# Three of four groups of a feed-forward projection computed as seven products of halves

## The chip, the core and the metric

The kernel runs on one core of one Trainium2 chip. The metric is the device time of one execution in microseconds (us): the median of several runs, lower is better. The engines are TensorE (PE; its weight loads are shown as PEld), VectorE (DVE), ScalarE (ACT), GpSimd (POOL) and SyncE (SP), whose queue here issues all DMA transfers. Each engine works through its own list of instructions in order; semaphores tie the lists together.

## The reference, cut to what matters

The model has two layers of width 1024 on 512 tokens, all in float32. Each layer mixes three branches (sparse attention, retention, a convolution) and ends with a feed-forward part, the only one that the change touches:

```python
for l in range(2):
    ...                                   # mixer: x = x + merged @ w_out[l]
    h2 = _rmsnorm(x, norm_mlp[l])         # (512, 1024)
    x = x + jnp.square(jax.nn.relu(h2 @ w_ff1[l])) @ w_ff2[l]   # 1024 -> 4096 -> 1024
return _rmsnorm(x, norm_final)
```

## The kernel before, in words

Activations lie transposed: a tile is 128 channels by 512 tokens, and `xT` is a list of eight of them. For float32 accuracy each operand of a product is split in a high part and the rest (`split`, lines 111 to 113: ScalarE rounds a copy `hi`, VectorE subtracts it from the source to give `lo`), and each product is three matmuls: high by high, high by low, low by high. A block of a projection (`proj`, lines 158 to 165) is one output tile of 128 channels: it goes over eight pieces k of 128 input channels, 24 matmuls of 512 columns into one PSUM tile `mm` (three buffers). Its weights come as one load of 512 KB into a tile `wr` (three buffers), are copied to `wh` by ScalarE (L145) and subtracted to `wl` by VectorE (L150 in this stage; elsewhere by GpSimd, L148).

The feed-forward stage (lines 795 to 819) has its operand `X` from `norm_split`: eight high/low pairs of `xT` times the gain of the norm; the row factor `rs` follows later and is multiplied in when a block is drained. The 4096 hidden channels are worked in four groups `q` of eight blocks. For each group the first projection makes eight blocks from `X` and `w_1`, each drained by VectorE (L806: relu, times `rs`), squared by ScalarE (L807) and split into a pair of hidden tiles; these lie in tiles `fa` of the stage's own pool in groups 0 and 2, and in tiles `bo` and `kv` of the mixer's pool in groups 1 and 3. Then the second projection makes eight blocks from `w_2` and the eight hidden pairs, and VectorE adds each to `xT[m]` (L817).

A scheduler of the framework puts each engine's instructions in an order of its own, from its own estimate of when each can start; tiles of one tag share a fixed number of buffers, and an instruction that takes a buffer again waits for its last reader.

Of the kernel before, what the change touches and what calls it, by code (L numbers as in the profile page):

```python
# [66 lines left out]
def block_kernel(ctx: ExitStack, tc: tile.TileContext, a, out):  # L67
    nc = tc.nc
    consts = ctx.enter_context(tc.tile_pool(name="consts", bufs=1))
    base = ctx.enter_context(tc.tile_pool(name="base", bufs=1))  # L70
# [12 lines left out]
    def tl(pool, tag, bufs, shape=(P, T), dtype=F):  # L83
        count[0] += 1
        return pool.tile(list(shape), dtype, name=f"{tag}_{count[0]}", tag=tag, bufs=bufs)

    def new_pool(name, side="left"):
        return tc.tile_pool(name=name, bufs=1, side=side, reuse_waits="tile")

    def tmp(shape=(P, T), dtype=F):  # L90
        return tl(base, "t", 3, shape, dtype)

    def small(shape, dtype=F):
        if math.prod(shape[1:]) <= 8:
            return tl(base, "n", 40, shape, dtype)
        return tl(base, "m", 7, shape, dtype)
# [11 lines left out]
    def mm(o, l, r, start, stop):  # L108
        return nc.tensor.matmul(o, l, r, start=start, stop=stop)  # L109

    def split(hi, lo, src, eng=None):
        nc.scalar.activation(hi, src, AF.Copy)
        return (eng or nc.vector).tensor_sub(lo, src, f(hi))
# [22 lines left out]
    def raw(srcs, nk, n):  # L136
        t = tl(base, "wr", 3, (P, nk, n))
        for dst, src in srcs(t):
            dma(dst, src)
        return t  # L140

    def wsplit(t, nk, n):
        h = tl(base, "wh", 3, (P, nk, n), FR)
        l = tl(base, "wl", 3, (P, nk, n), FR)
        nc.scalar.activation(h, t, AF.Copy)  # L145
        if lo_engine[0] is nc.gpsimd:
            for k in (slice(0, nk // 2), slice(nk // 2, nk)):
                nc.gpsimd.tensor_sub(l[:, k], t[:, k], f(h[:, k]))  # L148
        else:
            nc.vector.tensor_sub(l, t, f(h))  # L150
        return h, l

    def wblock(src, nk=KC, n=P):

        return wsplit(raw(lambda t: [(t, src)], nk, n), nk, n)

    def proj(o, w, x, nk=KC):

        h, l = w
        for k in range(nk):  # L160
            xh, xl = x[k]
            mm(o, h[:, k, :], xh, k == 0, False)
            mm(o, h[:, k, :], xl, False, False)
            last = mm(o, l[:, k, :], xh, False, k == nk - 1)
        return last
# [70 lines left out]
    first = start.enter_context(new_pool("first"))  # L236
    xT = [tl(first, "x0", 8) for _ in range(KC)]
    w_first = tl(base, "wr", 3, (P, KC, P))
    dma(pcol, a["cols"][:, 0:P])
    for c in range(KC):  # L240
        if c < 2:
            k = slice(4 * c, 4 * c + 4)
# [22 lines left out]
        for h in range(HEADS):  # L265
            dma(fd[h], f1[h:h + 1, :].to_broadcast([P, FLEN]))

    NR = 64
    open_pools = start
    for l in range(DEPTH):  # L270
        b = l * NR
        par = lambda at, n=1: pcol[:, b + at:b + at + n]
        w_f, w_t = a["w_f"][l], a["w_t"][l]

        if l == 0:
            h, lo = tl(base, "wh", 3, (P, KC, P), FR), tl(base, "wl", 3, (P, KC, P), FR)
# [3 lines left out]
        X, rs4, rs = norm_split(xT, par(0, 8), l == 0)  # L280
# [13 lines left out]
        def bo():  # L294
            return tl(mix_pool, "bo", 8, dtype=FR)

        def kv(shape=(P, T)):
            return tl(mix_pool, "kv", 12, shape, FR)
# [21 lines left out]
        def conv_taps_behind(ins, n):  # L320
            with tc.issue_after(ins.ins):
                conv_taps(n)
# [28 lines left out]
        for which, c0 in (("q", 0), ("k", 2)):  # L351
# [3 lines left out]
            for i in range(NB):  # L355
                z = pz[i].rearrange("p (h s d) -> p h s d", s=2, d=32)
                cosb = cs[:, i, None, None, 0:32].to_broadcast([P, 4, 2, 32])
                sinb = cs[:, i, None, 32:64].to_broadcast([P, 4, 32])
                A = tl(rp, "rr", 8, (P, 4, 2, 32))
                B = tmp((P, 4, 2, 32))  # L360
                nc.vector.tensor_mul(A, z, cosb)
                nc.vector.tensor_mul(B[:, :, 0, :], z[:, :, 1, :], sinb)
                nc.vector.tensor_mul(B[:, :, 1, :], z[:, :, 0, :], sinb)
                nc.vector.tensor_sub(A[:, :, 0, :], A[:, :, 0, :], B[:, :, 0, :])  # L364
                rotated = nc.vector.tensor_add(A[:, :, 1, :], A[:, :, 1, :], B[:, :, 1, :])
                rr.append(A)
                conv_taps_behind(rotated, T_ROT)
            for c in range(2):
# [4 lines left out]
                for s in range(2):  # L373
                    h = 2 * c + s
# [13 lines left out]
        for h in range(4):  # L388
            if h % 2 == 0:
# [16 lines left out]
            t = tmp()  # L406
# [7 lines left out]
            at = [slice(c, c + T - j * P) for j, c in enumerate((0, 512, 896, 1152))]  # L414
            for j in range(NB):
                n = T - j * P
                s = ps("sc")
                mm(s[:, :n], KSr[h][:, j * P:(j + 1) * P], QHr[h][:, j * P:], True, False)
                mm(s[:, :n], KSr[h][:, j * P:(j + 1) * P], QLr[h][:, j * P:], False, True)
                t = tl(rp, "rt", 2)  # L420
                nc.vector.tensor_mul(t[:, :n], s[:, :n], dec[:, :n])
                conv_taps_behind(split(ph[:, at[j]], pl[:, at[j]], t[:, :n]), T_SCORE)
            o = ps("av")
# [128 lines left out]
        for br, fb in ((0, FB_KS), (1, FB_KW)):  # L552
            pz = ps("mm")
            proj(pz, wblock(w_f[fb]), X)
            t = tmp()
# [13 lines left out]
        for i in range(NB):  # L569
# [4 lines left out]
                                                 op1=OP.subtract)  # L574
# [5 lines left out]
        def ut(dtype=F):  # L580
            return tl(cp, "u", 4, (P, T + CW - 1), dtype)[:, :T]
# [184 lines left out]
        for j in range(HPG):  # L766
            h, lo = tl(pp, "os", 8, dtype=FR), tl(pp, "os", 8, dtype=FR)
# [13 lines left out]
        for m in range(KC):  # L781
            h, lo = (bo(), bo()) if m < 4 else (kv(), kv())
            split(h, lo, merged[m])
            MG.append((h, lo))
        xT = []
        for m in range(KC):
            po = ps("mm")
            proj(po, wblock(a["w_o"][l, m]), MG)
            t = tl(a2, "on", 4) if m < 4 else tl(cp, "yc", 4)
# [7 lines left out]
        fp = phase.enter_context(new_pool(f"ff{l}"))  # L797
        X, rs4, rs = norm_split(xT, par(8, 8))
        lo_engine[0] = nc.vector
        for q in range(4):  # L800
            A = []
            for m in range(KC):
                pf = ps("mm")
                proj(pf, wblock(a["w_1"][l, q * KC + m]), X)
                t = tmp()
                nc.vector.scalar_tensor_tensor(t, pf, 0.0, rs, op0=OP.max, op1=OP.mult)  # L806
                nc.scalar.activation(t, t, AF.Square)  # L807
                if q % 2 == 0:
                    h, lo = tl(fp, "fa", 16, dtype=FR), tl(fp, "fa", 16, dtype=FR)
                else:  # L810
                    h, lo = (bo(), bo()) if m < 4 else (kv(), kv())
                split(h, lo, t)
                A.append((h, lo))
            for m in range(KC):
                pf = ps("mm")
                proj(pf, wblock(a["w_2"][l, q, m]), A)
                nc.vector.tensor_add(xT[m], xT[m], pf)  # L817
        phase.close()
        lo_engine[0] = nc.gpsimd

# [2 lines left out]
    for c in range(KC - 1):  # L823
        s = tmp()
# [4 lines left out]
    s = tmp()  # L829
# [59 lines left out]
```

## Time and profile before

| | |
|---|---|
| median of 3 runs | 1791.85 us (1791.27 to 1793.62) |
| profiled execution | 1793.25 us, span of its instructions 1791.5 us |
| TensorE busy | 1750.2 us, 98% of the span, granted clock 0.989 |
| VectorE, ScalarE, GpSimd busy | 1101.9, 775.0 and 504.8 us |
| feed-forward stages in the chain | 343.64 us from 564.49 us (layer 0), 343.97 us from 1437.13 us (layer 1) |

The span runs from the first to the last instruction; the execution's own time is 1.75 us longer. A matmul's own duration in the profile overlaps its neighbours', so the pace of TensorE is read from the starts of matmuls, not from their lengths. The same holds for VectorE and ScalarE where instructions stand queued.

### The profile page before, as it was taken

The page shows a single profiled execution, that of the slowest core. Times are in us where ns is not written, and L with a number is a line of the kernel's source. Part 1 is how long each engine was busy: PE and PEld are TensorE (multiplying, and loading weights), DVE is VectorE, ACT ScalarE, POOL GpSimd, SP SyncE. Part 2 cuts the span into 40 slices and gives each one's busy share as a digit, 9 for nine tenths or more (in the row PEclk, how much of TensorE's full clock was granted, in tenths as well). Part 3 has the DMA queues.
Part 4 walks back from the last instruction along what each step waited for, and adds up shares of the span by engine and source line. Part 5 has one row for each costly group of instructions (what it writes and reads, how often), then busy time and mean ns, then how long its engine had stood idle before and what let it go on. Part 6 is the DMA issues. An engine that isn't in the chain of part 4 may idle for free.

```text
span 1791.5 us, 23230 instructions
## 1 busy us (share of the span) xinstructions
PE 1750.2 (98%) x8592; PEld 1469.7 (82%) x8592; DVE 1101.9 (62%) x1979; ACT 775.0 (43%) x1421; POOL 504.8 (28%) x420
## 2 busy tenths in 40 slices
PE   8899899999999999999999999999999999999997
PEld 7788788887888888888898888888778888888886
DVE  6976978776764344434459768878768443434344
ACT  4433466675443232323434344667644442323241
POOL 4454444322581000000255544343327500000000
PEclk9999999999999999999999999999999999999999
DMA  4222623321553232333322232232236332332321
GB/s 166 89 86 64 198 95 107 112 95 65 205 184 105 94 94 94 96 95 101 133 101 89 89 119 92 95 126 98 83 122 227 122 94 95 94 96 93 106 85 69
DMA packets 70801, 195.82 MB, mean 109 GB/s; under 512 B 8944, under 2 KB 9328, under 8 KB 70688
## 3 DMA queue, kind: packets, MB, share of 16 engines
q1 hardware_dynamic: 70688, 194.34, 33.5%
q8 instruction: 68, 1.11, 0.3%
q14 instruction: 45, 0.37, 0.1%
HBM read 177.51 MB, written 19.42 MB: 110 GB/s over the span
## 4 chain that ended last, share of the span: by engine, by line
PE 68%; issue 20%; DVE 10%; ACT 1%; DMA 1%; SPq 0%; POOL 0%; POOLq 0%; DVEq 0%; ACTq 0%
PE mm L109 59%; PE sc L109 3%; PE av L109 3%; DVE yc L338 3%; PE tp L722 2%; PE tp L109 1%; DVE qk L386 1%; DVE XP L500 0%; DVE pc L684 0%; DVE rr L364 0%; DVE QS L657 0%; DVE s L712 0%; DVE pt L728 0%; DVE g L448 0%; DVE kv L563 0%
## 5 line engine op out<-in xcount | busy, mean ns | idle before, releaser
L109 PE MATMUL mm<-X,wh 128*128 128x512 f32 x2432 | 779.5, 396 | 12.5 <-ACT X L214 6.0
L148 POOL TENSOR_TENSOR wl<-wr,wh 128x512 fp32r<-128x512 f32 (+2 forms) x344 | 440.1, 1302 | 542.8 <-ACT wh L145 526.8
L145 ACT ACTIVATE wh<-wr 128x1024 fp32r<-128x1024 f32 (+2 forms) x301 | 296.0, 986 | 650.9 <-PE mm L109 522.1
L109 PEld LDWEIGHTS mm<-X,wh 128*128 128x128 f32 x2432 | 456.0, 190 | 102.2 <-ACT X L214 6.0
L109 PE MATMUL mm<-X,wl 128*128 128x512 f32 x1216 | 480.7, 395 | 0.0
L109 PEld LDWEIGHTS mm<-X,wl 128*128 128x128 f32 x1216 | 230.5, 190 | 45.3
L338 DVE SCALAR_TENSOR_TENSOR yc<-u,ccol,yc 128x512 f32<-128x512 f32 x240 | 213.0, 889 | 1.5
L150 DVE TENSOR_TENSOR wl<-wr,wh 128x1024 fp32r<-128x1024 f32 x129 | 158.1, 1226 | 38.2 <-ACT wh L145 38.2
L109 PE MATMUL mm<-bo,wh 128*128 128x512 f32 x512 | 160.6, 392 | 0.0
L109 PE MATMUL mm<-fa,wh 128*128 128x512 f32 x512 | 160.2, 395 | 0.0
L806 DVE SCALAR_TENSOR_TENSOR t<-mm,rs 128x512 f32<-128x512 f32 x64 | 43.9, 691 | 161.6 <-PE mm L109 156.1
L206 POOL TENSOR_TENSOR n<-n,mhalf 128x4 f32<-128x4 f32 x15 | 17.4, 1159 | 371.9 <-DVE n L204 371.9
L227 POOL TENSOR_TENSOR t<-t,t 128x512 f32<-128x512 f32 x18 | 27.4, 1523 | 333.7 <-DVE wl L150 314.4
L109 PE MATMUL mm<-kv,wh 128*128 128x512 f32 x384 | 119.7, 390 | 0.0
L109 PEld LDWEIGHTS mm<-fa,wh 128*128 128x128 f32 x512 | 96.1, 188 | 23.2
L109 PEld LDWEIGHTS mm<-bo,wh 128*128 128x128 f32 x512 | 96.1, 188 | 19.5
L728 DVE TENSOR_TENSOR pt<-tp,pt 128x256 fp32r<-128x256 f32 (+1 forms) x192 | 71.2, 375 | 65.0 <-ACT pt L727 64.3
L109 PE MATMUL mm<-fa,wl 128*128 128x512 f32 x256 | 100.6, 395 | 0.0
L109 PE MATMUL mm<-bo,wl 128*128 128x512 f32 x256 | 100.0, 391 | 0.0
L714 ACT ACTIVATE s<-s,n 128x128 f32<-128x128 f32 (+3 forms) x128 | 71.3, 558 | 43.9 <-DVE n L712 43.4
L109 PE MATMUL mm<-wh,X 128*128 128x256 f32 (+1 forms) x480 | 90.2, 287 | 0.0
L727 ACT ACTIVATE pt<-tp 128x256 fp32r<-128x256 f32 (+1 forms) x192 | 63.7, 340 | 58.6 <-PE tp L722 42.6
(219 smaller groups left out, 2417.9 us busy)
## 6 DMA issues: line engine op xcount, KB each, us to landing
wr<-in_w_dram SPq DMA_DIRECT2D x128, 512.0 KB, 3.6
wr<-in_w_f_dram SPq DMA_DIRECT2D x87, 512.0 KB, 3.3
wr<-in_w_b_dram SPq DMA_DIRECT2D x48, 256.0 KB, 2.7
wr<-in_w_t_dram SPq DMA_DIRECT2D x16, 512.0 KB, 3.4
gd<-g SPq DMA_DIRECT2D x32, 256.0 KB, 2.0
g<-gd SPq DMA_DIRECT2D x32, 256.0 KB, 4.1
wr<-in_w_o_dram SPq DMA_DIRECT2D x16, 512.0 KB, 3.6
md<-g SPq DMA_DIRECT2D x16, 256.0 KB, 2.9
```

What stands on the lines that cost most here:

```text
L109: return nc.tensor.matmul(o, l, r, start=start, stop=stop)
L145: nc.scalar.activation(h, t, AF.Copy)
L148: nc.gpsimd.tensor_sub(l[:, k], t[:, k], f(h[:, k]))
L150: nc.vector.tensor_sub(l, t, f(h))
L227: (nc.vector if c == KC - 1 or first_time else nc.gpsimd).tensor_add(s, s, acc)
L338: nc.vector.scalar_tensor_tensor(yc[c], x, w, yc[c], op0=OP.mult, op1=OP.add)
L386: nc.vector.tensor_sub(QLr[h][half], pt[nat], f(QHr[h][nat]))
L714: nc.scalar.activation(s, s, AF.Exp, scale=-1.0, bias=mx[:, i:i + 1], accum_out=den[:, i:i + 1])
L722: nc.tensor.transpose(pt[:, k * P:(k + 1) * P], cols[i][:, k * P:(k + 1) * P], ident)
L727: nc.scalar.activation(vh, src, AF.Copy)
L728: low = nc.vector.tensor_sub(vl, src, f(vh))
L806: nc.vector.scalar_tensor_tensor(t, pf, 0.0, rs, op0=OP.max, op1=OP.mult)
```

## The change

Group 0 of the first projection stays as it was. Groups 1, 2 and 3 are computed with a scheme of seven products of halves in place of eight (Strassen's in Winograd's form). The operand of a pair of blocks is cut in two: the input channels (`X[0:4]` and `X[4:8]`; of a weight block `lower` and `upper`) and the tokens (`left` and `right`, 256 each); the two output blocks of the pair are the two halves of the output channels. Each product has four pieces k, 12 matmuls of 256 columns, and goes into a PSUM tile of the tags `sc` and `tp` (two buffers each), which are free in this stage.

- `input_sums` makes, once per layer and beside group 0, the sums of the quarters of the operand, split into tiles `T`; the fourth sum overwrites the right halves of `X[0:4]` after group 0 has read them (`late`).
- `seven(q, p)` is a pair of blocks. It loads both raw weight blocks r1 and r2 into `wr`; r1 is split as before into `wh` and `wl` (A11 and A12 are its halves); VectorE makes four sums of weights in tiles `u` (128x512 each), and S1 to S4 and A22 (the upper half of r2) are split into pieces, 11 tiles of tags `kv` and `W` in rotation. Of the seven products ScalarE copies the first out of PSUM (`g`), and VectorE adds up the others into two output tiles (`t`), seven additions of 128x256. `done` then drains each as before.
- It is a generator: a pair's first four products stand ahead of the second projection's block m of the group before, two more behind that block, and the last behind block m + 1. So the first projection of group q + 1 is dealt out among the blocks of the second projection of group q.
- The hidden pairs lie in a ring of 30 tiles (14 `fa`, 8 `bo`, 8 `kv`).

```diff
+        spare = [kv() for _ in range(4)] + [tl(fp, "W", 7, dtype=FR) for _ in range(7)]
...
+        ring = [tl(fp, "fa", 14, dtype=FR) for _ in range(14)] + [bo() for _ in range(8)] + [kv() for _ in range(8)]
...
+        TS, late, kept = [], [], [ut(), ut()]
+
+        def input_sums(c):
+            b1, b2, s1, s2 = tl(base, "g", 3), tl(base, "g", 3), tmp(), tmp()[:, left]
+            nc.scalar.activation(b1, xT[c], AF.Copy, scale=par(8 + c))
+            nc.scalar.activation(b2, xT[c + 4], AF.Copy, scale=par(12 + c))
+            nc.vector.tensor_sub(s1[:, left], b1[:, right], b1[:, left])
+            nc.vector.tensor_sub(s1[:, right], b2[:, right], s1[:, left])
+            nc.vector.tensor_sub(s2, b2[:, right], b1[:, right])
+            h, lo = (tl(fp, "T", 8, (P, 3, HALF), FR) for _ in range(2))
+            last = kept[c // 2][:, (left, right)[c % 2]]
+            nc.vector.tensor_sub(last, b2[:, left], s1[:, right])
+            split(h[:, 0:2], lo[:, 0:2], s1)
+            split(h[:, 2], lo[:, 2], s2)
...
+            late.append((TS[-1][3], last))
+
+        def seven(q, p):
...
+            r1, r2 = (raw(lambda t: [(t, a["w_1"][l, q * KC + 2 * p + d])], KC, P) for d in range(2))
+            h1, l1 = wsplit(r1, KC, P)
+            s1, s2, s3, s4 = (ut().rearrange("p (k n) -> p k n", n=P) for _ in range(4))
...
+            def both(name, src):
+                W[name] = piece(), piece()
+                split(*W[name], src)
+
+            nc.vector.tensor_add(s1, r2[:, lower], r2[:, upper])
+            both("S1", s1)
+            nc.vector.tensor_sub(s2, s1, r1[:, lower])
+            both("S2", s2)
+            nc.vector.tensor_sub(s3, r1[:, lower], r2[:, lower])
+            nc.vector.tensor_sub(s4, r1[:, upper], s2)
+            both("S3", s3)
+            both("S4", s4)
+            both("A22", r2[:, upper])
...
+            def product(tag, w, B):
+                o = ps(tag)[:, :HALF]
+                h, lo = W[w]
+                for k, (bh, bl) in enumerate(B):
+                    mm(o, h[:, k], bh, k == 0, False)
+                    mm(o, h[:, k], bl, False, False)
+                    mm(o, lo[:, k], bh, False, k == 3)
+                return o
+
+            def done(y):
+                nc.vector.scalar_tensor_tensor(y, y, 0.0, rs, op0=OP.max, op1=OP.mult)
+                nc.scalar.activation(y, y, AF.Square)
+                h, lo = hidden_pair()
+                split(h, lo, y)
+                return h, lo
...
+            nc.scalar.activation(p1, product("sc", "A11", plain(0, left)), AF.Copy)
+            p5 = product("tp", "S1", turned(0))
+            add(y1[:, left], p1, product("sc", "A12", plain(4, left)))
+            add(u2, p1, product("tp", "S2", turned(1)))
+            add(u4, u2, p5)
+            yield
+            p7 = product("sc", "S3", turned(2))
+            add(u3, u2, p7)
+            add(y2[:, right], u4, p7)
+            add(y1[:, right], u4, product("tp", "S4", plain(4, right)))
+            out = [done(y1)]
+            yield
+            add(y2[:, left], u3, product("sc", "A22", turned(3)))
+            yield out + [done(y2)]
+
+        A = []
+        for m in range(KC):
+            A.append(first(0, m))
+            if m % 2:
+                input_sums(m // 2)
+        for (h, lo), t in late:
+            split(h, lo, t)
         for q in range(4):
-            A = []
-            for m in range(KC):
...
+            after = []
+            for m in range(0, KC, 2):
+                part = seven(q + 1, m // 2) if q < 3 else iter([None, None, []])
+                next(part)
+                second(q, m, A)
+                next(part)
+                second(q, m + 1, A)
+                after += next(part)
+            A = after
```

The changed lines move instructions on all engines, as the built programs show. Before, VectorE's list in this stage was, for a block of the second projection, the addition to `xT` (`on` or `yc`) and the `wl` of a later block, and nothing else:

```order
L817 TENSOR_TENSOR on_5162<-on_5162,mm_5789 128x512
L150 TENSOR_TENSOR wl_5889<-wr_5886,wh_5888 128x1024
L817 TENSOR_TENSOR on_5197<-on_5197,mm_5821 128x512
L150 TENSOR_TENSOR wl_5921<-wr_5918,wh_5920 128x1024
L817 TENSOR_TENSOR on_5232<-on_5232,mm_5853 128x512
```

Now 25 instructions stand there for two blocks. The rows below are the turn from one pair to the next in the middle of group 1 of layer 0 (L829 and L150: addition to `xT` and a `wl`; `kv_5488<-wr_7096`: the low half of A22 of the next pair; L911 and L890: the last addition and the drain of the pair at hand; L867 to L871: the weight sums S1 to S3 of the pair after next; L902 and L903: additions of products, `g` being half tiles of sums).

```order
L829 TENSOR_TENSOR on_5267<-on_5267,mm_7044 128x512
L150 TENSOR_TENSOR wl_7249<-wr_7246,wh_7248 128x1024
L113 TENSOR_TENSOR kv_5488<-wr_7096,kv_5487 128x512
L911 TENSOR_TENSOR t_6922<-g_6920,sc_7076 128x256
L890 SCALAR_TENSOR_TENSOR t_6922<-t_6922,rs_5478 128x512
L867 TENSOR_TENSOR u_7303<-wr_7297 128x512
L902 TENSOR_TENSOR g_7120<-g_7120,tp_7165 128x256
L113 TENSOR_TENSOR fa_5505<-t_6922,fa_5504 128x512
L869 TENSOR_TENSOR u_7304<-u_7303,wr_7295 128x512
L871 TENSOR_TENSOR u_7305<-wr_7295,wr_7297 128x512
L903 TENSOR_TENSOR g_7121<-g_7120,tp_7138 128x256
L113 TENSOR_TENSOR W_5490<-u_7303,W_5489 128x512
```

The sums of weights, which read raw tiles `wr`, now stand between additions that drain PSUM tiles. On the SP queue the loads follow each other as r1, r2 of a pair and the two blocks of the second projection beside it.

The second place is VectorE at the end of group 0 of layer 0, where the first pair of group 1 begins (`u_5899`: the fourth weight sum of the first pair, which reads its r1, `wr_5888`; L820: the drain of group 0's last block; L839 to L844: input sums of the last `c`; `wl_6043`: weights of the second projection's block 1; `W_5494<-wr_5890`: the low half of A22, from r2; `wl_6094`: the r1 of the second pair, `wr_6089`).

```order
L872 TENSOR_TENSOR u_5899<-wr_5888,u_5897 128x512
L820 SCALAR_TENSOR_TENSOR t_5859<-mm_5828,rs_5478 128x512
L839 TENSOR_TENSOR t_5866<-g_5864 128x256
L841 TENSOR_TENSOR t_5867<-g_5865,g_5864 128x256
L150 TENSOR_TENSOR wl_6043<-wr_6040,wh_6042 128x1024
L113 TENSOR_TENSOR W_5492<-u_5899,W_5491 128x512
...
L113 TENSOR_TENSOR W_5494<-wr_5890,W_5493 128x512
L113 TENSOR_TENSOR bo_5511<-t_5859,bo_5510 128x512
...
L113 TENSOR_TENSOR T_5874<-t_5867,T_5873 128x256
L150 TENSOR_TENSOR wl_6094<-wr_6089,wh_6093 128x1024
L113 TENSOR_TENSOR T_5874<-t_5866,T_5873 128x512
```

Before, two blocks' drains and splits and the first `wl` of the second projection stood there. The third place is TensorE a little later, within the first pair. Before, a second-projection block's 24 matmuls stood together; now the fourth k of the products S1 (`tp_5932`) and S2 (`tp_5959`), which reads the last `T` (`T_5873`), stands behind most of block 0 (`mm_5974`) and five matmuls of S3 (`sc_6006`).

```order
L109 MATMUL mm_5974<-bo_5510,wh_5977 128x512
L109 MATMUL sc_6006<-T_5609,W_5489 128x256
L109 MATMUL sc_6006<-T_5610,W_5489 128x256
L109 MATMUL sc_6006<-T_5609,W_5490 128x256
L109 MATMUL sc_6006<-T_5697,W_5489 128x256
L109 MATMUL sc_6006<-T_5698,W_5489 128x256
L109 MATMUL tp_5932<-T_5873,kv_5485 128x256
L109 MATMUL tp_5959<-T_5873,kv_5487 128x256
L109 MATMUL mm_5974<-bo_5511,wh_5977 128x512
```

Outside the two feed-forward stages TensorE's list is unchanged.

## Rows read from the trace of the kernel before

**Rows 1.** Page, head: busy us (share of the span) xinstructions of each engine.
```profile
PE 1750.2 (98%) x8592; PEld 1469.7 (82%) x8592; DVE 1101.9 (62%) x1979; ACT 775.0 (43%) x1421; POOL 504.8 (28%) x420
```

**Rows 2.** Chain that ended last, feed-forward of both layers: start us, us, engine, line.
```profile
564.49 343.64 PE mm L109 x1504
...
1437.13 343.97 issue
```

**Rows 3.** Stretches of layer 1's feed-forward: a first-projection group, a second-projection group.
```profile
core 0: us, PE busy (x) PEld busy (x) DVE busy (x) ACT busy (x) POOL busy (x), PEclk, DMA share, GB/s
...
1527.00:1569.00 42.00, 42.00 (x187) 34.81 (x186) 19.25 (x23) 16.24 (x22) 0.00 (x0) 1.00 0.28 88
1570.00:1612.00 42.00, 42.00 (x187) 34.81 (x186) 15.97 (x17) 9.67 (x10) 0.00 (x0) 1.00 0.33 101
```

**Rows 4.** Waits, layer 1's feed-forward: who for whom, us in total, times, longest.
```profile
DVE t L806 <- PE mm L109: 78.1, 29, 3.4
DVE yc L817 <- PE mm L109: 53.6, 16, 3.5
```

**Rows 5.** Timeline of TensorE, 512 and 256 columns: start us, us, instructions merged.
```profile
1454.67 0.62 PE L109 MATMUL mm<-X,wh 128*128 128x512 f32 x2
...
1455.35 0.62 PE L109 MATMUL mm<-X,wh 128*128 128x512 f32 x2
...
918.50 0.40 PE L109 MATMUL sc<-wh,X 128*128 128x256 f32 x2
...
918.86 0.40 PE L109 MATMUL sc<-wh,X 128*128 128x256 f32 x2
```

**Rows 6.** Timeline of VectorE, layer 1's feed-forward: drains and splits.
```profile
1442.87 1.89 DVE L806 SCALAR_TENSOR_TENSOR t<-mm,rs 128x512 f32<-128x512 f32 x3 [2.78 <-ACT rs L231]
...
1446.80 1.90 DVE L113 TENSOR_TENSOR fa<-t,fa 128x512 fp32r<-128x512 f32 x3 [0.85 <-ACT fa L112]
...
1465.75 0.69 DVE L806 SCALAR_TENSOR_TENSOR t<-mm,rs 128x512 f32<-128x512 f32 x1 [2.69 <-PE mm L109]
...
1487.98 0.69 DVE L817 TENSOR_TENSOR on<-on,mm 128x512 f32<-128x512 f32 x1 [3.51 <-PE mm L109]
...
1493.58 0.69 DVE L817 TENSOR_TENSOR on<-on,mm 128x512 f32<-128x512 f32 x1 [3.51 <-PE mm L109]
...
1586.71 0.69 DVE L817 TENSOR_TENSOR yc<-yc,mm 128x512 f32<-128x512 f32 x1 [3.35 <-PE mm L109]
...
1592.15 0.69 DVE L817 TENSOR_TENSOR yc<-yc,mm 128x512 f32<-128x512 f32 x1 [3.35 <-PE mm L109]
```

**Rows 7.** Groups by shape, VectorE in layer 1's feed-forward: busy us, mean ns.
```profile
L150 DVE TENSOR_TENSOR wl<-wr,wh 128x1024 fp32r<-128x1024 f32 x60 | 73.5, 1226 | 13.1 <-ACT wh L145 13.1
...
L113 DVE TENSOR_TENSOR fa<-t,fa 128x512 fp32r<-128x512 f32 x16 | 10.9, 691 | 0.9 <-ACT fa L112 0.9
```

**Rows 8.** Groups by shape, VectorE in the whole run, one of 256 elements.
```profile
L728 DVE TENSOR_TENSOR pt<-tp,pt 128x256 fp32r<-128x256 f32 x128 | 53.7, 419 | 46.8 <-ACT pt L727 46.2
```

**Rows 9.** Groups by shape, ScalarE in layer 1's feed-forward.
```profile
L145 ACT ACTIVATE wh<-wr 128x1024 fp32r<-128x1024 f32 x60 | 63.7, 1062 | 220.8 <-PE mm L109 220.8
L807 ACT ACTIVATE t<-t 128x512 f32<-128x512 f32 x32 | 19.6, 618 | 0.0
L112 ACT ACTIVATE fa<-t 128x512 fp32r<-128x512 f32 x16 | 9.9, 630 | 0.4
```

**Rows 10.** DMA issues in layer 1's feed-forward: KB each, median us to landing.
```profile
wr<-in_w_dram SPq DMA_DIRECT2D x57, 512.0 KB, 3.5
```

**Rows 11.** Page, DMA queues: packets, MB, share of 16 engines' span.
```profile
q1 hardware_dynamic: 70688, 194.34, 33.5%
```

**Rows 12.** DMA issues from 181 to 184 us, loads issued back to back.
```profile
w<-in_cmp_w_k_dram SPq DMA_DIRECT2D x2, 512.0 KB, 6.0
```

**Rows 13.** Timeline of TensorE, end of its longest idle stretch.
```profile
206.32 1.13 PE L109 MATMUL mm<-X,wh 128*128 128x512 f32 x2 [4.69 <-ACT G L575]
```

**Rows 14.** Stretches with a lower granted clock (columns as in rows 3).
```profile
206.50:209.80 3.30, 3.30 (x8) 2.55 (x9) 3.30 (x7) 1.67 (x5) 2.51 (x2) 0.50 1.02 328
...
1083.70:1090.50 6.80, 6.80 (x31) 6.70 (x31) 6.61 (x11) 1.62 (x5) 2.07 (x3) 0.50 0.57 186
```

More of the change, by code (lines that the diff above doesn't have):

```diff
@@ L266, in late_setup @@
             dma(fd[h], f1[h:h + 1, :].to_broadcast([P, FLEN]))
-    NR = 64
+    NR, HALF = 64, T // 2
     open_pools = start
@@ L799, in block_kernel @@
         lo_engine[0] = nc.vector
-        for q in range(4):
-            A = []
-            for m in range(KC):
[L803 to L817, printed above, removed]
+        left, right, lower, upper = slice(0, HALF), slice(HALF, T), slice(0, 4), slice(4, 8)
@@ new lines, in block_kernel, with piece, hidden_pair, first @@
+        spare = [kv() for _ in range(4)] + [tl(fp, "W", 7, dtype=FR) for _ in range(7)]
+        def piece():
+            spare.append(spare.pop(0))
+            return spare[-1].rearrange("p (k n) -> p k n", n=P)
+        def hidden_pair():
+            pair = ring[:2]
+            ring[:] = ring[2:] + pair
+            return pair
+        ring = [tl(fp, "fa", 14, dtype=FR) for _ in range(14)] + [bo() for _ in range(8)] + [kv() for _ in range(8)]
+        def first(q, m):
+            pf = ps("mm")
+            proj(pf, wblock(a["w_1"][l, q * KC + m]), X)
+            t = tmp()
+            nc.vector.scalar_tensor_tensor(t, pf, 0.0, rs, op0=OP.max, op1=OP.mult)
+            nc.scalar.activation(t, t, AF.Square)
+            h, lo = hidden_pair()
+            split(h, lo, t)
+            return h, lo
@@ new lines, in second @@
+        def second(q, m, A):
+            pf = ps("mm")
+            proj(pf, wblock(a["w_2"][l, q, m]), A)
+            nc.vector.tensor_add(xT[m], xT[m], pf)
+        TS, late, kept = [], [], [ut(), ut()]
[11 more added lines that the diff above has]
+            split(h[:, 2], lo[:, 2], s2)
+            TS.append([(h[:, i], lo[:, i]) for i in range(3)] + [tuple(x[:, right] for x in X[c])])
+            late.append((TS[-1][3], last))
@@ new lines, in seven @@
+        def seven(q, p):
+            r1, r2 = (raw(lambda t: [(t, a["w_1"][l, q * KC + 2 * p + d])], KC, P) for d in range(2))
+            h1, l1 = wsplit(r1, KC, P)
+            s1, s2, s3, s4 = (ut().rearrange("p (k n) -> p k n", n=P) for _ in range(4))
+            W = {}
+            def both(name, src):
[10 more added lines that the diff above has]
+            both("A22", r2[:, upper])
+            W["A11"], W["A12"] = ((h1[:, k], l1[:, k]) for k in (lower, upper))
+            plain = lambda at, t: [(h[:, t], lo[:, t]) for h, lo in X[at:at + 4]]
+            turned = lambda i: [t[i] for t in TS]
+            def product(tag, w, B):
[9 more added lines that the diff above has]
+                nc.scalar.activation(y, y, AF.Square)
+                h, lo = hidden_pair()
+                split(h, lo, y)
+                return h, lo
+            add = nc.vector.tensor_add
+            p1, u2, u3, u4 = (s for t in (tl(base, "g", 3), tl(base, "g", 3)) for s in (t[:, left], t[:, right]))
+            y1, y2 = tmp(), tmp()
+            nc.scalar.activation(p1, product("sc", "A11", plain(0, left)), AF.Copy)
[12 more added lines that the diff above has]
+            yield out + [done(y2)]
@@ new lines, in block_kernel @@
+        A = []
[4 more added lines that the diff above has]
+        for (h, lo), t in late:
+            split(h, lo, t)
+        for q in range(4):
+            after = []
[7 more added lines that the diff above has]
+            A = after
```

## The prediction

> **What bounds the kernel now.** I read the head of the page first: TensorE is busy for 98% of the span, VectorE for 62%, ScalarE for 43% [rows 1]. So the time is TensorE's, unless something makes it wait. The chain that ended last says the same of the two feed-forward stages, the only stretches that change: from 564.49 us it is 343.64 us of matmuls of L109, and from 1437.13 us it is one entry of 343.97 us of "issue", in which nothing is waited for [rows 2]. The table of stretches shows the stage from inside: TensorE is full at clock 1.00 in groups of both projections, while VectorE works 19.25 of 42 us in a first-projection group and 15.97 of 42 in a second, ScalarE 16.24 and 9.67, GpSimd not at all [rows 3]. The waits of this stage are VectorE's for TensorE's blocks [rows 4].
>
> Two prices follow. In the timeline of TensorE three matmuls of 512 columns start every 0.68 us (1454.67, 1455.35), 0.2267 us each; three of 256 columns every 0.36 us (918.50, 918.86), 0.120 us each [rows 5]. Half the columns save 0.107 us, so some 13 ns of each matmul do not shrink with its columns. Seven eighths of the columns in more matmuls are therefore worth less than an eighth.
>
> **What the change takes away and adds on TensorE.** I call the work on one pair of output blocks a part: 4 pairs, 3 groups, 2 layers, 24 parts. A pair was 2 x 24 matmuls of 512 columns, 48 x 0.2267 = 10.88 us; it becomes 7 x 12 of 256 columns, 84 x 0.120 = 10.08 us. That is 0.80 us a part and 19.2 us in all. The Trainium skill (TensorE: Matmul & The Clock Gate, "Back-to-back issue gap") gives N/2.4 + 2.5 ns; by it the gain would be 48 x 0.2158 - 84 x 0.1092 = 1.19 us a part, an estimate of 28.5 us. The rows show 13 ns in place of its 2.5; both sizes are measured here, so this result gets no chance.
>
> Something may be taken back. The blocks of the second projection come 5.60 us apart where they read `fa` tiles and 5.44 us apart where they read `bo` and `kv` [rows 6]: 6.7 ns more a matmul for operands in the feed-forward's own pool. The new `T` and `W` tiles lie in that pool too. No row has a 256-column matmul with such operands, so the bounds are nothing and 6.7 ns on all 60 matmuls of a part that read `T` or `W` (0.40 us). I take half of it on the 36 that stream `T`, since they have half the columns: 0.12 us a part, 2.9 us in all.
>
> **The other engines, steady state.** A part now lasts TensorE 10.08 + 0.12 + two blocks of the second projection (10.88 to 11.20), 21.1 to 21.4 us. VectorE has in it 15 instructions of 512 elements (0.69 us), 7 of 256 (0.42) and 3 of 1024 (1.23): 17.0 us busy [rows 7, 8]. Queued without a wait they start closer together: three of 512 take 1.90 us, so one starts 0.605 us after another [rows 6], which is 0.085 less than its length; I take 0.335 and 1.19 for the other two sizes. ScalarE has about 9 us [rows 9]. All seven weights of a part are made one part ahead, so what VectorE is late by does not reach TensorE at once.
>
> But there is a ring through the three `wr` buffers. The last reader of the raw block r2 is the low half of A22, which VectorE does after the A22 product of the part before (`kv_5488<-wr_7096` in the excerpt from the middle of group 1). Only then may SP issue the next r1, and behind it the next r2; the third row after it on VectorE (`u_7303<-wr_7297`) waits for that r2, and everything queued behind it (the drains `g_7120`, `t_7122` of the products too). A load takes 3.5 us to land [rows 10]. For a second one behind it I add 1.6: all transfers together moved 194.34 MB in 33.5% of 1791.5 us, 1.62 us for 512 KB [rows 11]. So `u_7303` starts about 5.2 us after the end of A22's low half. Then, to the next one: 14 of 512 elements 8.47, 6 of 256 2.01, 3 of 1024 3.57, the tail and two results needed at once 0.3, and one detour over ScalarE (Square and copy, 0.62 + 0.63, with handovers 1.4) [rows 9]: 15.7 us. The ring takes 20.9 us, just under TensorE's 21.1. The upper bound, no overlap at all (17.2) and a second load of 6.0 (the median of two issued back to back at 181.8 [rows 12]), is 23.3. I take 20.9, as the instructions are those of this stage and their overlap is shown; on that value the ring costs nothing.
>
> **The way in.** The first group stays in 512 columns, but VectorE must also make `T`, the sums of the first seven, and overwrite halves of `X`. From the end of the wait for `rs` (1442.87) to the end of the group's last block (about 1471.2, 5.44 after the one before at 1465.75) there are 28.3 us [rows 6]; up to the fourth weight sum (`u_5899`, in the excerpt from the end of group 0) stand 24 instructions of 512, 18 of 256 and 5 of 1024, 14.5 + 6.0 + 6.0 = 26.5 us, and with some 3.5 us of waits for ScalarE's copies it ends about 1.7 us after the last block (Z + 1.7). Its end frees a `wr` buffer: the load for the second projection's next block lands at Z + 5.3, ScalarE's copy of it (1.06 [rows 9]) ends at 6.4, four shorter copies queued behind it at 8.5, the low half of A22 (`W_5494<-wr_5890`) at 9.3. That frees r2: the next r1 lands at 12.9, its copy ends at 14.0, and behind it on ScalarE stands the high half of the last `T` (`T_5873`), 14.6. TensorE meanwhile does 42 matmuls of 256 (5.04), 22 of the second projection (5.1) and 5 of S3 (0.6): at Z + 10.8 it comes to the row `tp_5932<-T_5873` and waits 3.8 us. Bounds: nothing, if VectorE is 2 us quicker and a load shorter, and 7 us. Twice, 7.6 us. It also leaves VectorE about 0.9 us further behind TensorE, with 1.4 us in hand before the drain of A22 (needed 36 x 0.12 = 4.3 us into a part) would hold A12 up.
>
> **Hidden at no cost:** the extra copies of `xT` on ScalarE (blocks of 5.44 us cover 0.63 each); the hidden ring of 15 pairs (the sixteenth pair overwrites the first of the group that has been read); the last pair of a group (ready some 8 us into the next part, read by the eighth k, at 5.8 + 4.8 = 10.5). The last is the nearest: with VectorE over 2.5 us later TensorE would wait for the rest, once a group.
>
> **Sum.** -19.2 + 2.9 + 7.6 = -8.7 us. On the profiled execution's own 1793.25 that is 1784.5; the median of the runs is 1791.85, 1.4 lower, and I give 1783.
>
> **Rivals.**
> *The ring binds (slower).* For: the ring is only 0.2 to 0.5 us shorter than TensorE's part, and it runs through a pair of loads, a detour over ScalarE and 23 queued instructions; 30 ns more at each decides. Against: VectorE's rows show it keeping 0.605. Each us over TensorE's part costs 11 x 1 - 1.4 = 9.6 us a layer. It eats the 8.7 from 0.53 us over (a ring of 21.7) and turns slower by 0.2% at 0.7; at 22.3, 1.0 over 21.3, it gives -8.7 + 19.2, 1802; at its bound of 23.3, 1824.
>
> *The way in and the operands cost nothing.* For: the waits on loads are my chain of ten steps, any of which may be shorter. Then 16 to 19 us are gained: 1773 to 1776.
>
> *The clock falls in the way in.* For: after the one idle stretch of 4.69 us on TensorE, which ended at 206.32, the clock stood at 0.50 from 206.5 to 209.8 and eight matmuls filled 3.3 us [rows 13, 14]: 1.65 us lost. Another fall in this trace lasted 6.8 us [rows 14], 3.4 lost. Against: TensorE is full on both sides of the wait of 3.8 us. Twice 1.7 to 3.4 on top: 1786.6 to 1790. The Trainium skill (same page, "HAM oscillation — how this bites in real kernels") says that waits between bursts of matmuls bring the clock back to half; the trace agrees for the wait of 4.69 us.
>
> **Chances.** The sum as worked out, TensorE's pace with the wait on the way in: 0.43, 1778 to 1788. No cost on the way in: 0.10. The clock falls as well: 0.18. The ring binds: 0.29. What this measurement can tell from no change is about 0.2%, 3.6 us. Faster: 0.41 of the first, all of the second, 0.06 and 0.03 of the others, 0.60. The same: 0.02 + 0.11 + 0.04, 0.17. Slower: 0.01 + 0.22, 0.23. The range leaves about 0.1 out at each end: from 1774, which cuts off the best of the second case, to 1800, a ring of about 22.2.
>
> **What would show it.** Right: 84 matmuls of 256 columns starting 0.120 to 0.124 us apart; second-projection blocks of the same group pair 21.1 to 21.4 us apart; one wait of TensorE of 2 to 5 us per layer at `tp<-T`, released by ScalarE or VectorE; VectorE waiting at L867 for a load of `wr` for some 4 us in every part. Wrong: waits of TensorE on A12, S4 or the `mm` blocks for VectorE drains in every part (the ring binds); a part above 21.8 us; a clock under 1.00 after the first group; 256-column matmuls over 0.13 us apart.

## The result and the profile after

The change makes the kernel 1.1% faster: 1772.5 us median (1771.53 to 1777.85, 4 runs) against 1791.56 of the kernel before on the same chip, ratio 0.9892, 95% interval 0.988 to 0.9904. That is 19.1 us, where 8.7 were forecast; the median lies 1.5 us under the low end of the range. The profiled execution took 1772.18 us, its span is 1770.4.

The head of the page after, to read beside [rows 1]:

```profile
PE 1729.6 (98%) x9456; PEld 1492.7 (84%) x9456; DVE 1276.7 (72%) x2395; ACT 853.0 (48%) x1581; POOL 502.9 (28%) x420
```

VectorE has 175 us more to do, ScalarE 78 us, and TensorE is as full as before. The chain that ended last (start us, us, what) answers to [rows 2]:

```profile
562.87 28.91 PE mm L109 x127
...
648.25 5.58 PE mm L109 x24
653.83 2.85 PE sc L109 x24
656.68 2.87 PE tp L109 x24
...
669.40 5.58 PE mm L109 x24
...
690.48 5.48 PE mm L109 x24
...
711.47 5.48 PE mm L109 x24
...
845.15 51.41 PE mm L109 x225
...
1425.91 334.00 issue
```

Layer 1's stage is again one entry in which nothing is waited for, 334.00 us for 343.97. Layer 0's runs from 562.87 to 845.15 + 51.41 = 896.56, 333.69 us for 343.64. Together they give 19.9 us, so the whole gain is made here, and TensorE makes it. The entries in between show the parts. From the second block of one pair to that of the next are 21.15 us where the blocks read `fa` (669.40 - 648.25) and 20.99 where they read `bo` and `kv` (711.47 - 690.48); without the two blocks of the second projection 10.0 us are left for 84 products of 256 columns. Twenty-four of these take 2.85 to 2.87 us, 0.119 us each, whether they stream `X` or `T`.

The stretch of four parts (columns as in [rows 3]) and VectorE's waits in it (who for whom, us in total, times, longest):

```profile
1516.00:1600.00 84.00, 84.00 (x528) 75.97 (x528) 61.66 (x101) 36.31 (x52) 0.00 (x0) 1.00 0.31 101
```

```profile
DVE u L867 <- DMA wr<-in_w_dram: 8.3, 4, 2.1
DVE yc L829 <- PE mm L109: 3.6, 4, 1.4
DVE on L829 <- PE mm L109: 3.3, 4, 1.3
DVE fa L113 <- ACT fa L112: 2.7, 2, 1.4
DVE kv L113 <- ACT kv L112: 2.7, 2, 1.4
DVE wl L150 <- ACT wh L145: 1.4, 8, 0.2
```

VectorE now works 15.4 of the 21 us of a part and idles 5.6. Some 2 us of that are its wait for the second raw weight, where it starts the weight sums of the next part (8.3 us in the four parts); the rest are waits for TensorE's blocks (6.9) and for ScalarE's copies (6.8). TensorE has no wait in either stage, on the way in neither.

The way in, layer 0: the timeline of all engines (start us, us, engine, line; in brackets the idle time before and its releaser). The first group's last block ends and A11 begins at 591.62, which is the Z of the prediction:

```profile
587.97 1.22 DVE L150 TENSOR_TENSOR wl<-wr,wh 128x1024 fp32r<-128x1024 f32 x1
...
589.22 4.35 SPq L139 DMA_DIRECT2D wr<-in_w_dram  x2
...
591.62 0.40 PE L109 MATMUL sc<-X,wh 128*128 128x256 f32 x2
...
592.52 0.69 DVE L872 TENSOR_TENSOR u<-wr,u 128x512 f32<-128x512 f32 x1
...
592.70 1.06 ACT L145 ACTIVATE wh<-wr 128x1024 fp32r<-128x1024 f32 x1 [1.91 <-DMA wr<-in_w_dram]
...
593.23 4.27 SPq L139 DMA_DIRECT2D wr<-in_w_dram  x3
...
596.46 0.69 DVE L113 TENSOR_TENSOR W<-wr,W 128x512 fp32r<-128x512 f32 x1
...
596.79 1.06 ACT L145 ACTIVATE wh<-wr 128x1024 fp32r<-128x1024 f32 x1 [0.36 <-DMA wr<-in_w_dram]
...
597.76 0.62 ACT L112 ACTIVATE T<-t 128x512 fp32r<-128x512 f32 x1
...
599.47 0.69 DVE L113 TENSOR_TENSOR T<-t,T 128x512 fp32r<-128x512 f32 x1
...
602.34 0.39 PE L109 MATMUL tp<-T,kv 128*128 128x256 f32 x2
```

The fourth weight sum (L872) ends at Z + 1.6, 0.1 us before its forecast. But ScalarE's copy of the weights of the second projection's next block starts at 592.70, Z + 1.1, where the forecast had them land at Z + 5.3: that load was issued at 589.22, when the split of the block before it (L150) had given its own raw weights back, 4 us ahead of the fourth sum's end. The buffer of the sum goes to the next part's r1, issued at 593.23 and landed at 596.79, 7.7 us ahead of the forecast. The low half of A22 (`W<-wr`, 596.46) ends at Z + 5.5, where 9.3 was forecast. The last pieces of `T` are written at 600.2, 2.2 us before TensorE comes for them at 602.34; that moment, Z + 10.7, is again within 0.1 us of the forecast.

### The profile page after: what moved, and what is told of

It is laid out like the page before. It is cut to its first block, busy times and chain, and to the rows that moved or that the text cites. A ratio compares the mean times of both kernels' runs of the same rounds, so it can differ in the third digit from the quotient of the medians.

```text
span 1770.4 us, 25533 instructions
## 1 busy us (share of the span) xinstructions
PE 1729.6 (98%) x9456; PEld 1492.7 (84%) x9456; DVE 1276.7 (72%) x2395; ACT 853.0 (48%) x1581; POOL 502.9 (28%) x420
## 4 chain that ended last, share of the span: by engine, by line
PE 69%; issue 20%; DVE 8%; ACT 1%; DMA 1%; POOL 0%; SPq 0%; POOLq 0%; DVEq 0%; ACTq 0%
PE mm L109 52%; PE sc L109 7%; PE tp L109 4%; PE av L109 3%; DVE yc L338 2%; PE tp L722 2%; DVE qk L386 1%; POOL wl L148 0%; DVE kv L563 0%; ACT wh L145 0%; DVE rr L364 0%; DVE rr L365 0%; PE tp L190 0%; DMA g<-gd 0%; DVE s L712 0%
## 5 line engine op out<-in xcount | busy, mean ns | idle before, releaser
L109 PE MATMUL mm<-X,wh 128*128 128x512 f32 x1664 | 543.0, 399 | 11.7 <-ACT X L214 5.8
L145 ACT ACTIVATE wh<-wr 128x1024 fp32r<-128x1024 f32 (+2 forms) x277 | 270.4, 979 | 388.8 <-PE mm L109 251.4
L109 PEld LDWEIGHTS mm<-X,wh 128*128 128x128 f32 x1664 | 311.6, 191 | 72.4 <-ACT X L214 6.4
L109 PE MATMUL mm<-X,wl 128*128 128x512 f32 x832 | 330.9, 398 | 0.1
L109 PEld LDWEIGHTS mm<-X,wl 128*128 128x128 f32 x832 | 158.2, 190 | 30.8 <-DVE wl L150 0.6
L150 DVE TENSOR_TENSOR wl<-wr,wh 128x1024 fp32r<-128x1024 f32 x105 | 128.5, 1224 | 29.4 <-ACT wh L145 29.1
L109 PEld LDWEIGHTS mm<-kv,wh 128*128 128x128 f32 x384 | 72.1, 188 | 16.2 <-ACT kv L112 1.2
```

## The experiments

All stage times below are the one "issue" entry of layer 1 in each run's chain. Each ratio is to the kernel before as it was measured beside that run (medians of 1791.56 to 1793.31 us).

| run | median us | ratio to before (95%) | stage of layer 1 |
|---|---|---|---|
| before, after | 1791.56, 1772.5 | 0.9892 (0.988 to 0.9904) | 343.97, 334.00 |
| e1_rotate | 1774.17 | 0.9899 (0.9885 to 0.9913) | 334.17 |
| e8_late5 | 1771.73 | 0.9889 (0.9866 to 0.9911) | 334.01 |
| e9_late10 | 1776.34 | 0.9906 (0.9884 to 0.9927) | 334.23 |
| e2_vec4 | 1770.81 | 0.9892 (0.9869 to 0.9915) | 334.00 |
| e3_vec8 | 1796.23 | 1.0017 (1.0008 to 1.0026) | 344.95 |
| e4_no_group | 1794.25 | 1.0009 (1.0 to 1.0019) | 344.33 |
| e4_one_group | 1789.64 | 0.9985 (0.9975 to 0.9996) | 340.70 |
| e10_last_group | 1790.21 | 0.9989 (0.9979 to 1.0) | 340.94 |
| e5_apart | 1783.81 | 0.9956 (0.9939 to 0.9973) | 337.45 |
| e7_before_padded | 1782.86 | 0.9948 (0.993 to 0.9966) | 341.37 |
| e6_after_padded | 1766.05 | 0.985 (0.9838 to 0.9863) | 332.25 |

The medians are coarser than some forecasts below: e1 lies 1.7 us over the changed kernel's median and e2 1.7 us under it, outside the 1 and 1.5 us that they name, and e4_no_group 2.8 us over 1791.5, outside its 2 us. Their stages of layer 1 differ by 0.36 us or less from the kernel that they are compared with, so these runs are read by the stage.

Theory: TensorE's pace alone sets the stage, and the wait on the way in is missing because a load takes the buffer that was given back first, while the prediction had the three `wr` buffers go round in strict turn. Rivals: something else hides late loads; the ring through VectorE is close to binding; part of the gain comes from the new order and not from the fewer columns.

**e1_rotate: the buffers in strict turn.**
```diff
-        t = tl(base, "wr", 3, (P, nk, n))
+        turn[0] += 1
+        t = tl(base, f"wr{turn[0] % 3}", 1, (P, nk, n))
```


> The three raw-weight buffers are forced into strict rotation, everything else as in the changed kernel. If the only fault of the prediction was the order in which these buffers are reused, its wait on the way in appears now: 3.8 us in each layer, so +7.6 us and about 1780, with the steady parts still at TensorE's 21.0 to 21.2 us, since the ring was put at 20.9. Rival one, something else than the buffers' order hides the late loads: within 1 us of 1772.5. Rival two, rotation makes the ring itself too long: each of the 24 parts longer by 0.5 to 2 us, 1784 to 1820.

Measured: no wait of TensorE; the stage is 334.17 us. The load for block 1 is as late as the prediction had it, and yet nothing waits. Timeline of this run (its line numbers are 6 higher, and its A11 begins at 592.46, its Z):

```profile
597.51 1.06 ACT L151 ACTIVATE wh<-wr 128x1024 fp32r<-128x1024 f32 x1
598.48 0.61 ACT L112 ACTIVATE T<-t 128x512 fp32r<-128x512 f32 x1
...
601.82 1.06 ACT L151 ACTIVATE wh<-wr 128x1024 fp32r<-128x1024 f32 x1 [2.42 <-DMA wr<-in_w_dram]
...
600.11 0.68 DVE L113 TENSOR_TENSOR T<-t,T 128x512 fp32r<-128x512 f32 x1
...
603.63 0.40 PE L109 MATMUL tp<-T,kv 128*128 128x256 f32 x2
```

The next block's weights are copied at 597.51, Z + 5.0, which is 4.0 us later than in the run above. But the order of the built program has changed with the edit: the last copy into `T` now stands ahead of the copies that have to wait (601.82), so `T` is whole at 600.8, and TensorE comes for it at 603.63. The copy at 601.82 is that of the next r1; it starts at Z + 9.4, late, but not as late as the forecast's landing at Z + 12.9, as the low half of A22 comes earlier in this order too (at Z + 5.0, where 9.3 was forecast). So the buffers' order is not the whole cause: the engines' lists changed with it. Rival one holds on the stage. That the scheduler moved the copy because it reckons with the return of the buffer is inferred; this run shows only that it did.

**e8_late5, e9_late10: the first buffer of the way in given back later.**
```diff
-            nc.vector.tensor_sub(s4, r1[:, upper], s2)
+            for _ in range(6 if (q, p) == (1, 0) else 1):      # e9: 11
+                nc.vector.tensor_sub(s4, r1[:, upper], s2)
```


> The fourth weight sum of the first part of each layer is made six times over in place of once, 5 x 0.69 = 3.5 us of VectorE, so that the first raw weight of that part gives its buffer back 3.5 us later and all that the built order has behind it on the way in comes later. If the way in has only the 2.1 us of room that the trace of the changed kernel shows (last pieces of T written at 600.2 us, needed at 602.3): +1.4 us a layer in the feed-forward stage, +2.8 in all, and the wait stands on TensorE there. Rival, the order of the built program is drawn again around the later sum and hides it: each layer's stage within 0.3 us of the changed kernel's.

> The same with eleven sums in place of one, 6.9 us. With 2.1 us of room: +4.8 us a layer, +9.6 in all, about 1782. Rival, hidden by the order drawn again: each layer's stage within 0.3 us of the changed kernel's.

Measured: stages of 334.01 and 334.23 us, against 334.00; no wait of TensorE in layer 0's stage either. The rival holds: 3.5 and 6.9 us of lateness are hidden, because the copy of r1 and three of e8's six and eight of e9's eleven repeated sums now stand behind the pieces of `T`. e9's median is 3.8 us higher than the changed kernel's, its stage only 0.23, and the intervals overlap. What the wait would cost with the order held fixed was not tried: each of the three edits that make a load late drew the order again.

**e2_vec4, e3_vec8: more work for VectorE in every part.**
```diff
-            nc.vector.tensor_sub(s3, r1[:, lower], r2[:, lower])
+            for _ in range(5):                                 # e3: 9
+                nc.vector.tensor_sub(s3, r1[:, lower], r2[:, lower])
```


> Four extra copies of the third weight sum in each part, 4 x 0.69 = 2.8 us of VectorE a part. If TensorE's pace alone sets a part and VectorE's idle time (about 5.6 us a part after the change, 2.0 of it the wait for a raw weight) is real room: no change, within 1.5 us of 1772.5. Rival, the ring stands at the 20.9 us of the prediction, 0.2 under TensorE: +2.6 us a part, +62 us, about 1834.

> Eight extra copies of the third weight sum in each part, 5.5 us of VectorE a part. If the room is the 5.6 us of idle time less the 2.0 us for the raw weight that no order can remove, 3.6 us: over by 1.9 us a part, +46 us, about 1818. If all of the idle time can be filled: no change. Rival, a ring of 20.9 us: +5.3 us a part, +127 us, about 1900.

Measured: four more cost nothing, 334.00 us again; eight more cost 10.95 us a layer, 0.91 us a part, and turn the gain into 0.2% slower. The stretch of four parts in e2, and then entries of e3's chain (L872 is the repeated sum there):

```profile
1516.00:1600.00 84.00, 84.00 (x529) 76.04 (x528) 72.74 (x122) 36.49 (x53) 0.00 (x0) 1.00 0.32 103
```

```profile
646.52 1.24 DVE wl L150
...
647.77 3.52 DMA wr<-in_w_dram
...
718.92 0.70 DVE u L872
...
719.63 3.45 DMA wr<-in_w_dram
...
723.11 0.69 DVE u L867
...
1439.93 344.95 issue
```

In e2 VectorE is busy for 72.74 of 84 us, 11.1 us more than after the change, and TensorE still for all of them. e2 came as the theory had it; of e3's three forecasts none did, though the 0.91 lies between no change and the 1.9 of its first case. In e3 the loads of `wr` are on the chain, so a ring through them binds, but it is not the ring of the prediction: of the eight loads on the chain in layer 0's stage four begin when a split of weights (L150) has given a raw tile back and four when a repeated sum has, since these sums read the raw tiles too; none begins behind the low half of A22. Queued sums start 0.605 us apart [rows 6] and last 0.69, so eight add 4.8 to 5.5 us, of which 0.91 show. If the sums did nothing but take VectorE's time, there were 3.9 to 4.6 us of room in a part and VectorE's round takes about 16.5 to 17.2 us after the change; that is an estimate. e2 by itself shows 2.4 us of room (four at 0.605) or more. Both are against a ring of 20.9 us.

**e4_no_group, e4_one_group, e10_last_group: how many groups in seven products.**
```diff
+        def twice(q, p):
+            out = [first(q, 2 * p)]
+            yield
+            yield
+            yield out + [first(q, 2 * p + 1)]
-                part = seven(q + 1, m // 2) if q < 3 else iter([None, None, []])
+                part = (seven if q < 1 else twice)(q + 1, m // 2) if q < 3 else iter([None, None, []])
```
The line shown is that of one group; with none it is `twice` throughout, with the last `seven if q == 2`. In the runs with one group the plain groups read `X` after the fourth input sum has taken the place of half of four of its tiles: the same instructions on other numbers.

> The changed kernel's order and its ring of hidden tiles, but every group of the first projection in the eight products of before (no seven-product form, no sums of weights or inputs); the pairs of blocks are dealt among the second projection's blocks. If the whole gain is TensorE's 0.80 us a part: as before, 1791.5 within 2 us. Rival, the dealing itself gives part of the 19 us: 1780 to 1787.

> Seven products for the second group of each layer alone (8 parts), the third and fourth group in the form of before, dealt out in the same way. If the gain is 0.80 us a part and nothing is paid once per layer: 8 x 0.80 = 6.4 us, about 1785. Rival, a cost paid once per layer (the way in) is hidden in the 19 us and each part gives more than 0.80: with 3.8 us a layer the gain here would be (19.1 + 7.6) / 3 - 7.6 = 1.3 us, about 1790.

> Seven products for the fourth group of each layer alone (8 parts), the second and third group in the form of before, dealt out. By TensorE's pace: 4 parts a layer, each 0.80 to 0.92 shorter, so the stage 3.2 to 3.7 us a layer shorter than with no group in seven products, and the whole about 1787. The way into the first part now lies a long time after the input sums, so a cost of the way in, if there is one in the run with the second group alone, would be gone here: rival, 1 us or more a layer better than that run.

Measured on the stage: none 344.33, the second alone 340.70, the last alone 340.94, three 334.00. So the new order alone costs 0.36 us a layer and gives nothing; one group gives 3.63 or 3.39 us, three give 10.33, which is 0.85 to 0.91 us a part and proportional to the parts. A cost paid once on the way in would show as a worse first group; the second group alone is 0.24 us better than the last alone. On the stage's time all three rivals fall. The medians do not say so by themselves: 1789.64 for the second group alone is the rival's 1790 and not the 1785 of eight parts, and the two runs with one group are 4.6 and 4.0 us better than none, where two stages say 7. The rest of the kernel differs from run to run by some 3 us: with the second group alone, layer 0's stage (564.70 to 905.09) is 3.2 us shorter than before, and yet layer 1's begins at 1436.98, where it began at 1437.13 [rows 2].

**e5_apart: the dealing undone.**
```diff
-            for m in range(0, KC, 2):
-                part = seven(q + 1, m // 2) if q < 3 else iter([None, None, []])
-                next(part)
-                second(q, m, A)
-                next(part)
-                second(q, m + 1, A)
-                after += next(part)
+            for m in range(KC):
+                second(q, m, A)
+            for p in range(KC // 2 if q < 3 else 0):
+                after += list(seven(q + 1, p))[2]
```


> The changed kernel with the dealing undone: all eight blocks of the second projection of a group first, then the four parts of the next group one after the other. If VectorE's work on a part (about 15.5 us) is only hidden because two blocks of the second projection lie beside it: a part by itself is bound by VectorE, 15.5 us to 19 us with the wait for the raw weights, against 10.1 of TensorE, so +5.4 to +9 us for each of the 24 parts, +130 to +215 us, 1900 to 1990. Rival, VectorE is no limit: within 2 us of 1772.5.

A miss on both sides: 337.45 us, 3.45 us a layer slower than dealt out, nowhere near the 65 to 107 that were expected. The table of stretches in layer 0 (columns as in [rows 3]) shows why:

```profile
589.70:634.40 44.70, 44.70 (x195) 36.14 (x194) 25.90 (x37) 14.46 (x20) 0.00 (x0) 1.00 0.29 95
634.40:664.50 30.10, 29.08 (x241) 28.68 (x241) 26.44 (x48) 15.74 (x26) 0.00 (x0) 1.00 0.27 88
664.50:720.30 55.80, 55.77 (x291) 47.32 (x290) 35.06 (x53) 19.10 (x28) 0.00 (x0) 1.00 0.35 110
```

The timeline of TensorE at the end of the second of them:

```profile
662.93 1.59 PE L109 MATMUL tp<-X,W 128*128 128x256 f32 x12
664.35 0.62 PE L109 MATMUL mm<-bo,wh 128*128 128x512 f32 x2
664.82 1.59 PE L109 MATMUL sc<-X,W 128*128 128x256 f32 x12
```

The scheduler does not follow the code's order. The first blocks of the next second projection (`mm<-bo`) begin at 664.35, while products of the last parts are still to come, and so cover VectorE's work on them. Over the 85.9 us of the second and third stretch VectorE is busy for 61.5, as much as when dealt out; only in the short stretch is it nearly full (26.44 of 30.1), and there TensorE idles for 1.0 us.

**e6_after_padded, e7_before_padded: where the tiles begin.** In the trace of after, blocks on `fa` take 5.58 us and those on `bo` and `kv` 5.48. All tiles that are placed behind the gate tile `G` of 384 bytes a partition, `fa`, `T` and `W` among them, begin 128 bytes past a multiple of 256 in the built program; `X`, `bo` and `kv` begin on one.
```diff
-        G = tl(mix_pool, "G", 1, (P, NB, 24))
+        G = tl(mix_pool, "G", 1, (P, NB, 32))[:, :, :24]
```


> The changed kernel with the gate tile G padded from 384 to 512 bytes a partition, so that all tiles placed behind it start on a multiple of 256 bytes; the program is the same instruction for instruction. If the place of the moving operand is why the blocks on fa tiles take 5.58 us and those on bo and kv 5.44 to 5.48: all blocks at 5.45, 717 products of 512 columns 6.6 ns shorter, -4.7 us, and some more where other stages use such tiles: 1763 to 1768. Rival, the place is nothing and the blocks differ for another reason: within 1 us of 1772.5.

> The kernel before with the gate tile G padded from 384 to 512 bytes a partition. If the place of the moving operand makes the blocks on fa tiles longer: 768 products of 512 columns 6.6 ns shorter, -5.1 us, and some more elsewhere, 1782 to 1786.5. Rival, the place is nothing: within 1 us of 1791.5.

Measured: 1766.05 and 1782.86 us. The chain of e6, from the same place as that of after above:

```profile
645.35 5.47 PE mm L109 x24
650.82 2.87 PE sc L109 x24
653.69 2.88 PE tp L109 x24
...
666.35 5.47 PE mm L109 x24
...
1420.02 332.25 issue
```

All blocks take 5.47 us now, whichever tiles they read. The 256-column products take 2.87 to 2.88 for 24, no less than before the padding: the place costs them nothing. e6 is the fastest version: the changed kernel with padding, 1.5% under the kernel before. With both kernels padded the stage goes from 341.37 to 332.25, 9.12 us a layer or 0.76 a part.

## Why the prediction was wrong

**TensorE's saving: right.** 0.80 us a part were forecast, 0.83 came (9.97 us a layer for 12 parts): against the order without seven products it is 0.86, as a product of 256 columns starts every 0.119 us and not every 0.120, and the new order takes back 0.36 us a layer. The Trainium skill (TensorE: Matmul & The Clock Gate, "Back-to-back issue gap") would have made it an estimated 28.5 us by N/2.4 + 2.5 ns, which it gives as the gap of an isolated matmul and calls too long for a stream of 512 columns; here it is too short, 215.8 ns for 226.7, and the two stages gave 19.9 us. Two products of 256 columns at 0.119 cost 11 ns more than one of 512 at 0.2267, and the rows decide.

**The operands' place: a term of 2.9 us that is zero for products of 256 columns.** The prediction carried half of the 6.7 ns of a 512-column matmul over to products of 256 columns. With `T` at either place 24 of them take 2.85 to 2.88 us, and padding does not shorten them.

**The way in: the step that failed.** It stands in the prediction as "Its end frees a `wr` buffer: the load for the second projection's next block lands at Z + 5.3". The sum's end was right to 0.1 us, but that load had the buffer of the block before it, given back some 4 us earlier, and the sum's buffer went to the next r1, for which the prediction waited until the low half of A22. Each load was put one release too late, so the last high half of `T_5873` was copied at Z + 14.6 in the text and at Z + 6.8 in the trace (597.76 + 0.62), and the wait of 3.8 us, twice, did not come: 7.6 us. With the 2.9 us of the operands that is, to 0.1 us, what the forecast of 8.7 us fell short of 19.1. e1 shows a second fault behind the first. With the buffers in strict turn the load for block 1 is as late as forecast, and still there is no wait, since the order changes with it. In all three runs with a late load (e1, e8, e9) the copy of r1 stands behind the last `T`; the order that the prediction read, with the copy ahead of it, belongs to the program in which r1 comes early. Whether that order with late loads would have cost the 3.8 us stays open.

**The ring: hidden, as forecast, but by estimate 2 to 4 us too long.** 20.9 us were worked out; e2 leaves some 18.6 or less of TensorE's 21.0 if its four sums all stand in the ring, and e3's estimate is 16.5 to 17.2. (VectorE is busy for 15.4 us of a part where the sum of single lengths made it 17.0, since queued instructions overlap.) The fault is that of the way in: the prediction lets the low half of A22 release the next r1, with the next r2 behind it. The timelines of VectorE and of the SP queue after the change show other releases:

```profile
688.53 1.23 DVE L150 TENSOR_TENSOR wl<-wr,wh 128x1024 fp32r<-128x1024 f32 x1 [0.17 <-ACT wh L145]
689.78 0.33 SPq L139 DMA_DIRECT2D wr<-in_w_dram  x1
...
696.86 1.23 DVE L150 TENSOR_TENSOR wl<-wr,wh 128x1024 fp32r<-128x1024 f32 x1 [0.17 <-ACT wh L145]
698.00 0.69 DVE L113 TENSOR_TENSOR W<-wr,kv 128x512 fp32r<-128x512 f32 x1
698.11 0.33 SPq L139 DMA_DIRECT2D wr<-in_w_dram  x1
698.72 0.33 SPq L139 DMA_DIRECT2D wr<-in_w_dram  x1
...
701.75 0.69 DVE L867 TENSOR_TENSOR u<-wr 128x512 f32<-128x512 f32 x1 [2.00 <-DMA wr<-in_w_dram]
```

The next r1 is issued at 689.78 and the next r2 at 698.11, each when a split (L150) has given back the raw weights of a block of the second projection. What the low half of A22 gives back at 698.69 goes to the load of 698.72, in the built program that of a later block of the second projection. So the sum that waits for r2 starts 3.6 us after r2's issue and 3.1 us after the end of A22's low half, not 5.2, and VectorE idles for 2.0 of these. The chance of 0.29 for this rival was too high for a ring with this much room; that the ring as drawn can bind at all, no run shows.

**The clock.** The granted clock is 1.00 in the stretch of four parts; as TensorE had no wait on the way in, that rival's condition never came about, and no run here shows what it would have cost.

So the case to which the prediction gave 0.10, no cost on the way in and none for the operands, is the one that came: 16 to 19 us, against 19.1.

## What to carry to other kernels

When TensorE is full and waits for nothing, a change of its work is worth what its own starts say, form by form; a cost added on top needs a row of its own. Before a late load is charged, find out which release its buffer comes from; where a scheduler writes the order, an edit that makes a load late changes the order too. The room of a hidden engine is measured by adding work to it until the time moves: here four sums a part were free and eight were not; the added work must not hold buffers that the unchanged program gives back earlier.

## What the runs showed of the hardware that was not expected

A matmul of 512 columns is slower when its moving operand begins 128 bytes past a multiple of 256 than when it begins on one: 5.58 to 5.60 us for 24 against 5.44 to 5.47, some 5 to 7 ns each, while products of 256 columns take the same at either place (2.85 to 2.88 us for 24). Other offsets were not tried. One padded tile, no instruction changed, brought the kernel before from 1792.12 to 1782.86 us (0.9948, 0.993 to 0.9966); 2.60 us of it lie in each feed-forward stage (343.97 to 341.37), the rest in other stages, which were not taken apart.
